# The first expert's extra rows ahead of its gate, and linear attention with unmasked keys: one layer of a hybrid diffusion block on one Trainium2 core

## The chip, the core and the metric

The kernel runs on one core of one Trainium2 chip. The metric is device time in microseconds, from launch to end, as the median of several runs. Of the kernel before there are three runs: 1279.64, 1281.47 and 1281.56 us, so the median is 1281.47 us. One execution was also taken with the hardware profiler; all views below come from that one.

## The reference, cut to what matters

256 tokens of width 1024 and 256 context tokens go through one layer, in float32. First a mixer: a combined input projection (`w_in`), then two branches, a bidirectional chunked gated linear attention (4 heads, keys of 64, values of 128, chunks of 64 tokens) and a latent attention, a merge with sigmoid gates, and an output projection. Then a mixture of 32 experts, of which each token takes its top 4.

```python
ds = jnp.einsum("bhncd,bhnce->bhnde", k_to_end, vc)      # state added by one chunk of 64 tokens
def step(s, inp):
    d, dsn = inp
    return d[..., None] * s + dsn, s
...
merged = jax.nn.sigmoid(f["zm_gla"]) * br_gla + jax.nn.sigmoid(f["zm_mla"]) * br_mla
...
mod_x = jnp.split((jax.nn.silu(c) @ w_mod[l] + b_mod[l])[:, None, :], 6, axis=-1)
...
for e in range(N_EXPERTS):
    gate = jnp.minimum(tok @ p["w_gate"][e] + p["b_gate"][e], SWIGLU_LIMIT)
    up = jnp.clip(tok @ p["w_up"][e] + p["b_up"][e], -SWIGLU_LIMIT, SWIGLU_LIMIT)
    act = (up + 1.0) * gate * jax.nn.sigmoid(SWIGLU_ALPHA * gate)
    out = out + combine[:, e:e + 1] * (act @ p["w_down"][e] + p["b_down"][e])
```

## The kernel before, in words

**Loads.** Nearly all weights come in pieces of 2 MB, issued by SyncE (SP) in its program order. In the mixer the class `Slots` (L90) holds three slots; `PLAN` (L27) says which piece goes into which slot and in which order, and `done(name)` frees a slot and issues what is next for it (L115). All four pieces `g0` to `g3` of the modulation weights use slot 2, one after the other. For the experts the class `Ring` (L48) has ten slots: each expert has two pieces of its gate, two of its up and two of its down projection, and `done(n)` frees the n oldest pieces and issues as many new ones (L75), each of which waits for TensorE's last read of its slot.

**Mixer.** `work()` (L604) yields the projection products piece by piece; each `Q(...)` (L864) in the linear attention flushes stored evacuations, runs one such product step (24 matmuls of 256 columns, high and low parts of the split weights), splits the next weights (`wsh` on ScalarE L365, `wsl` on VectorE L366), and may then take one half of a `g` piece: `mod_part` (L313) scales 2 times 128x1024 on ScalarE (L322) and adds them on GpSimd (L324). TensorE, VectorE, ScalarE, GpSimd and SP follow the written order there.

Linear attention: `decays(t)` (L911) makes the decay factors and the keys `kx`, one masked tile for each chunk with the other chunk's 64 rows at zero (L930 to L932); `states(i)` (L944) multiplies keys and values chunk by chunk and adds to the running state (L954); `queries`, `scores`, `inner`, `outer` follow. The order of the stretch is: decays(0), Q, decays(1), Q, states(0), queries(0), states(1), Q, states(2), then scores and inner products with Qs between them. Halves of `g1` are taken by the second and third Q, those of `g2` by two Qs after `queries(1)`. `on_pool` (L846) prepares the bias rows `RB` on GpSimd.

**Experts.** Tokens of an expert are gathered into 64 slots; an expert with more than 64 tokens has 32 extra rows, under `tc.If(rv > 0)`, where `rv` is loaded by every engine from the tile `trips` (L1573, L1589). `project` (L1437) multiplies gathered rows with the pieces, `gated` and `upped` evacuate, `turn` transposes, `down` multiplies with the down pieces, `scatter` adds to the output accumulators. Expert 0 is written out by hand (L1613 to L1645): main gate products with the extra rows' gather between them, `table()`, the slots' tokens, the gate, then the extra rows' gate products in two halves, each of which frees one piece; likewise up and down. Experts 1 to 31 (L1647 to L1656): gate, up, then under the `If` the extra rows' gather, gate and up, and only then `ring.done(4)`; after the down products `ring.done(2)`. After expert 20 a loop for crowded experts is skipped over (`crowded`, L1534).

Of the kernel before, what the change touches and what calls it, by code (L numbers as in the profile page):

```python
# [17 lines left out]
D = 1024  # L18
# [4 lines left out]
EB = 2  # L23
LIMIT = 7.0
# [103 lines left out]
def block_kernel(ctx: ExitStack, tc: tile.TileContext, a, out):  # L128
# [185 lines left out]
    def mod_part(name, jj, done=True):  # L314

        c, acc, first = int(name[1]), sums[name[0]], name[1] == "0" and jj == 0
        if jj == 0:
            sums[name] = ring.take(name)
        w = sums[name][:, jj]
        for n in range(2):  # L320
            v, to = w[:, ts(n, 1024)], acc[:, ts(n, 1024)]
            nc.scalar.activation(to if first else v, v, AF.Identity, scale=cz[:, 2 * c + jj, 0:1])  # L322
            if not first:
                nc.gpsimd.tensor_add(to, to, v)  # L324
        if jj == 1 and done:
            ring.done(name)
# [285 lines left out]
    def work():  # L612
# [22 lines left out]
        for n in range(6):  # L635
# [203 lines left out]
    kx = [[place(2, 1536 + 1024 * t + 512 * c, 512, 2) for c in range(2)] for t in range(2)]  # L839
# [3 lines left out]
    bias_dma = nc.sync.dma_start(bias[:96], a["b_gu"].rearrange("k p n -> p k n"))  # L843
    side = []

    def on_pool():  # L846

        nc.gpsimd.memset(RB, 0.0)
        yield
        for k in range(2):  # L850
            for h in range(2):
                v, part = bias[:, k, ts(h, 512)], RB[:, k, ts(h, 512)]
                mid, low = slice(32, 64), slice(64, 96)
# [36 lines left out]
    for t in range(2):  # L890
        for c in range(2):
            nc.gpsimd.memset(kx[t][c][64 * (1 - c):64 * (1 - c) + 64], 0.0)
# [20 lines left out]
    def decays(t):  # L913
# [16 lines left out]
        for c in range(2):  # L930
            r = slice(64 * c, 64 * c + 64)
            nc.vector.tensor_mul(kx[t][c][r], er[r], zk[r, t:t + 1].to_broadcast([64, 2, 256]))  # L932
# [3 lines left out]
    Q(1, "g1:0")  # L936
# [4 lines left out]
    Q(1, "g1:1")  # L941


    def states(i):  # L944
        ps_ = []
        for d in range(2):
            c = i if d == 0 else 3 - i
            p = bank(f"p_ds{d}{i}", (128, 2, 2, 128))
            ds_mm(p, kx[c // 2][c % 2], c // 2, d, None, None)
            ps_.append((p, c))  # L950
# [20 lines left out]
    last_e = nc.scalar.activation(sg, zg, AF.Sigmoid)  # L971
# [55 lines left out]
    Q(1)  # L1027
    inner(0, 0)
    scores(0, 1)
    Q(1)  # L1030
# [75 lines left out]
    for b, o, name in ((1, om, "w_br_mla"), (0, og, "w_br_gla")):  # L1106
        w = w_br.pop(name, None) or ring.take(name)
        for c in range(4):
# [8 lines left out]
            with tc.issue_after(last_e.ins):  # L1117
                nc.scalar.activation(v, v, AF.Sigmoid)
# [26 lines left out]
    comb3 = late.tile([128, 2, 96], F32, name="comb3")  # L1145
# [180 lines left out]
    def slot_ids(at, slots):  # L1326

        return iota[:, at:at + slots].unsqueeze(1).to_broadcast([128, 128 // slots, slots])

    def select(G, i, e):  # L1330

        for t in range(2):
            nc.vector.tensor_scalar(G[:, t, i], slot_ids(0, SLOTS), posm[:, t, e:e + 1], r2[t], op0=ALU.is_equal, op1=ALU.mult)

    def gather(X, G, g):

        p = bankb("p_xg", (128, 4, SLOTS * EB))
        for k in range(4):
            for t in range(2):
                mm(p[:, k], x1[:, t, ts(4 * g + k, 128)], G[:, t, :, 0], t == 0, t == 1)  # L1340
# [8 lines left out]
    def gather_one(X, G, i):  # L1349

        p = bankb("p_xg")
        for t in range(2):
            for q in range(2):
                mm(p[SLOTS * q:SLOTS * q + SLOTS], G[:, t, i, 0], x1[:, t, ts(q, 512)], t == 0, t == 1)
        yield
        xg = [mo.tile([128, 512], F32, tag=n, name="xg")[:, :256] for n in "su"]
# [20 lines left out]
    def table():  # L1377
# [5 lines left out]
        for t in range(2):  # L1383
            nc.tensor.transpose(p[:96, 2 + t], comb3[:, t], C("ident"))
        q = p.rearrange("p a b -> p (a b)")
        v, part = q[:, 256:], where[:, 256:]
        mid, low = slice(32, 64), slice(64, 96)
        nc.scalar.copy(where[:32, :256], q[:32, :256])
        nc.vector.tensor_copy(part[:96], v[:96])
        nc.vector.tensor_sub(part[mid], v[mid], part[mid])  # L1390
        nc.vector.tensor_sub(v[low], v[low], part[low])
        nc.vector.tensor_copy(part[low], v[low])
# [15 lines left out]
    def block_tiles():  # L1408
        return (mo.tile([128, 2, EB, 128 // SLOTS, SLOTS], F32, tag="G", name="G"),
                mo.tile([128, 8, EB * SLOTS], F32, tag="X", bufs=2, name="X"))  # L1410

    def more_gather(at, posm, tag="1"):

        rep = 128 // MORE
        G = mo.tile([128, 2, rep, MORE], F32, tag="G" + tag, name="G")
        for t in range(2):
            nc.vector.tensor_scalar(G[:, t], slot_ids(at, MORE), posm[:, t], r2[t], op0=ALU.is_equal, op1=ALU.mult)
        yield None
        p = bankb("p_xg", (128, D // rep))
        for t in range(2):  # L1420
            for q in range(rep):
                mm(p[MORE * q:MORE * q + MORE], G[:, t, 0], x1[:, t, ts(q, D // rep)], t == 0, t == 1)
        xg = mo.tile([128, 512], F32, tag="s", name="xg")[:, :D // rep]
# [35 lines left out]
    def more_bank(k):  # L1459
        return bankb(f"p_m{k}", (128, 256))  # L1460
# [11 lines left out]
    def more_in(of, X, W, w):  # L1472

        p = more_bank(0)
        project(0, p, of, X, 0, W, MORE)
        g = more_gated(p, w)
        p = more_bank(1)
        project(1, p, of, X, 0, W, MORE)
        return more_upped(p, g)
# [46 lines left out]
    def more_out(S, ps_, ns=range(2)):  # L1526

        ys = [halves(p, (("g", "s"), ("u", "y1"))[n]) for n, p in zip(ns, ps_)]
# [3 lines left out]
    def crowded():  # L1532

        with tc.If(worst > 1):  # L1534
            with tc.For_i(0, NE, 1) as ev:
# [8 lines left out]
                with tc.For_i(1, rv, 1):  # L1544
# [9 lines left out]
                    u2 = more_in(se, X2, lambda c, j: rows_from(("w_gate", "w_up")[c // 2], 4 * (c % 2) + j), w2)  # L1554
# [7 lines left out]
    select(G, 0, 0)  # L1562
    first = gather_one(X, G, 0)
    next(first)
# [9 lines left out]
    steps = [more_gather(SLOTS, posm[:, :, 0:1])]  # L1574
    next(steps[0])
    next(first)
    next(first)
    softmax(0, 1)
    softmax(1, 1)
    nc.vector.tensor_copy(comb3.rearrange("p t (c e) -> p t c e", c=3), comb.unsqueeze(2).to_broadcast([128, 2, 3, 32]))  # L1580
    select(G, 1, 1)
    chain.__exit__(None, None, None)
    ctx.enter_context(tc.manual_schedule(engines={E.PE}))
# [15 lines left out]
    for e in range(NE):  # L1599
# [12 lines left out]
        u = mo.tile([128, 512], F32, tag="u", name="u")  # L1612
        if e == 0:  # L1613

            project(0, p, of, X, 0, W, SLOTS, range(0, 4))
            steps.append(next(steps[0]))
            project(0, p, of, X, 0, W, SLOTS, range(4, 6))
            X1 = next(steps[0])
            table()
            project(0, p, of, X, 0, W, SLOTS, range(6, 8))  # L1620
            toks[0] = slot_tokens(of, first_sid)
            gated(p, g, toks[0][1])
            p1 = more_bank(0)
            for half in range(2):
                with tc.If(rv > 0):
                    if half == 0:
                        S1, w1 = slot_tokens(of, more_sid, "1")
                    project(0, p1, of, X1, 0, W, MORE, range(4 * half, 4 * half + 4))
                    if half:
                        g1 = more_gated(p1, w1)  # L1630
                ring.done(1)
                rv = blocks(e, ring.last.ins)
            p = bankb("p_up", tag="g")
            p1 = more_bank(1)
            for half in range(2):
# [8 lines left out]
                ring.done(1)  # L1644
                rv = blocks(e, ring.last.ins)  # L1645
        else:
            project(0, p, of, X, SLOTS * i, W, SLOTS)  # L1647
            gated(p, g, toks[e][1])
            p = bankb("p_up", tag="g")
            project(1, p, of, X, SLOTS * i, W, SLOTS)  # L1650
            upped(p, g, u)
            with tc.If(rv > 0):  # L1652
                X1 = list(more_gather(SLOTS, posm[:, :, e:e + 1]))[-1]
                S1, w1 = slot_tokens(of, more_sid, "1")
                u1 = more_in(of, X1, W, w1)
            ring.done(4)  # L1656
        following = list(range(e - i + EB, e - i + 2 * EB))
        if e and following[0] < NE:
# [5 lines left out]
            if i == 1:  # L1664
                gather(Xn, Gn, 1)
        aT = turn(u, SLOTS)
        if e:
            scatter(*todo)
        else:
            nxt = gather_one(X, G, 1)  # L1670
            for _ in range(3):
                next(nxt)
# [218 lines left out]
```

## Time and profile before

| | us |
|---|---|
| median of three runs | 1281.47 (1279.64 to 1281.56) |
| the profiled execution, device time | 1282.0 |
| its span, first to last instruction | 1280.1 |
| TensorE matmuls busy | 1153.5 (90% of the span) |
| VectorE, ScalarE, GpSimd busy | 420.8, 255.6, 133.5 |
| read from memory | 460.27 MB |

The span starts with the first instruction; 1.9 us of the execution lie around it. Times in the views are microseconds from the span's start. A busy TensorE is not TensorE at its peak; what counts in a stretch is which wait ends last there.

### The profile page before, as it was taken

The numbers are of one execution on the slowest core, as the hardware profiler recorded it, in microseconds if no ns is written. First come the engines' busy times: TensorE is split into PE (matmuls) and PEld (weight loads), VectorE is DVE, ScalarE is ACT, GpSimd is POOL, SyncE is SP. The second block draws the span as 40 slices with busy tenths as digits, with TensorE's granted clock in tenths as the row PEclk, the third lists the DMA queues.
The fourth block names the chain that finished last, engine by engine and source line by source line (L and its number), as shares of the span: only waits on it lengthen the run. The fifth ranks groups of instructions, "written<-read, shape, count | busy, mean of one in ns | idle before, by whom it ended". The sixth has DMA issues, their size and how long they took to land. (4 is left out here: it accounts for less than half of the span.)

```text
span 1280.1 us, 16131 instructions
## 1 busy us (share of the span) xinstructions
PE 1153.5 (90%) x6486; PEld 612.0 (48%) x6487; DVE 420.8 (33%) x784; ACT 255.6 (20%) x437; POOL 133.5 (10%) x93
## 2 busy tenths in 40 slices
PE   8999979999899999998988899998969889999984
PEld 5776768886344444443433343443524334444421
DVE  5667576685421222211111222221212111121212
ACT  4556534543111010110001010100101000110101
POOL 2346236540000000000000000000000000000000
PEclk9999989999999999999999999999989999999997
DMA  9843445896669999999999999999889999999993
GB/s 364 321 167 112 193 154 191 344 352 269 264 233 425 426 426 426 425 425 428 425 426 427 427 425 425 426 425 426 378 372 425 427 425 428 424 427 426 425 413 128
DMA packets 37988, 463.24 MB, mean 362 GB/s; under 512 B 4600, under 2 KB 4856, under 8 KB 10336
## 3 DMA queue, kind: packets, MB, share of 16 engines
q1 hardware_dynamic: 37424, 461.16, 86.6%
q8 instruction: 100, 1.64, 0.5%
q14 instruction: 32, 0.26, 0.1%
q10 hardware_dynamic: 432, 0.18, 0.1%
HBM read 460.27 MB, written 1.05 MB: 360 GB/s over the span
## 5 line engine op out<-in xcount | busy, mean ns | idle before, releaser
L203 PE MATMUL p_up<-w,X 128*64 128x512 f32 x1024 | 229.5, 594 | 15.8 <-DMA w<-in_w_up_dram 15.8
L203 PE MATMUL p_y<-w,aT 128*64 128x512 f32 (+1 forms) x1088 | 236.1, 599 | 1.0 <-ACT aT L1487 1.0
L203 PE MATMUL p_gate<-w,X 128*64 128x512 f32 x1024 | 230.1, 597 | 3.3 <-DMA w<-in_w_gate_dram 3.3
L203 PEld LDWEIGHTS p_up<-w,X 128*64 128x64 f32 x1024 | 88.5, 137 | 144.6 <-issue 111.6
L203 PEld LDWEIGHTS p_gate<-w,X 128*64 128x64 f32 x1024 | 95.7, 138 | 114.4 <-issue 108.1
L203 PEld LDWEIGHTS p_y<-w,aT 128*64 128x64 f32 (+1 forms) x1088 | 72.7, 136 | 144.0 <-issue 141.3
L213 POOL TENSOR_TENSOR rx<-rx,cst 128x1 f32<-128x1 f32 x2 | 1.5, 770 | 965.3 <-DVE rx L212 965.3
L1510 DVE TENSOR_TENSOR yl<-p_y,yh 128x512 fp32r<-128x512 f32 x33 | 22.8, 691 | 227.6 <-ACT yh L1509 227.6
L1451 DVE TENSOR_SCALAR g<-p_gate 128x512 f32<-128x512 f32 x32 | 22.1, 692 | 218.5 <-PE p_gate L203 218.5
L203 PE MATMUL p_xg<-G,x 128*128 128x128 f32 x480 | 64.8, 290 | 32.0 <-PEq L1652 20.4
L203 PEld LDWEIGHTS p_xg<-G,x 128*128 128x128 f32 x480 | 59.2, 200 | 56.9 <-issue 56.9
L1487 ACT COPY aT<-p_aT 128x512 f32<-128x512 f32 (+1 forms) x34 | 19.5, 575 | 322.7 <-PE p_aT L1485 322.7
L1456 DVE TENSOR_SCALAR u<-p_up 128x512 f32<-128x512 f32 x32 | 22.1, 692 | 171.6 <-PE p_up L203 171.6
L1452 ACT ACTIVATE s<-g 128x512 f32<-128x512 f32 (+1 forms) x34 | 21.0, 617 | 285.7 <-DVE g L1451 285.7
L1509 ACT CAST yh<-p_y 128x512 fp32r<-128x512 f32 x33 | 19.4, 587 | 212.9 <-PEq L1709 199.6
L203 PE MATMUL p_gate<-h0h,wsl 128*128 128x256 f32 x160 | 47.1, 294 | 4.5 <-DVE wsl L366 4.3
L203 PEld LDWEIGHTS <-selb 128*64 128x64 bf16 (+2 forms) x178 | 15.4, 104 | 72.9 <-issue 67.4
L203 PE MATMUL p_gate<-h0h,wsh 128*128 128x256 f32 x160 | 48.7, 304 | 0.0
L1346 DVE TENSOR_SCALAR X<-p_xg,mA_gpref,mB_gpref 128x128 f32<-128x128 f32 x60 | 24.6, 410 | 71.8 <-PE p_xg L203 53.7
L203 PE MATMUL p_gate<-h0l,wsh 128*128 128x256 f32 x160 | 46.8, 292 | 0.0
L324 POOL TENSOR_TENSOR sums<-sums,g 128x1024 f32<-128x1024 f32 x14 | 37.2, 2682 | 60.4 <-ACT g L322 60.4
L366 DVE TENSOR_TENSOR wsl<-p,wsh 128x1024 fp32r<-128x1024 f32 x27 | 39.4, 1462 | 9.8 <-ACT wsh L365 9.7
(437 smaller groups left out, 1480.0 us busy)
## 6 DMA issues: line engine op xcount, KB each, us to landing
w<-in_w_gate_dram SPq DMA_DIRECT2D x64, 2048.0 KB, 35.8
w<-in_w_up_dram SPq DMA_DIRECT2D x62, 2048.0 KB, 35.8
w<-in_w_down_dram SPq DMA_DIRECT2D x62, 2048.0 KB, 27.9
p<-in_w_in_dram SPq DMA_DIRECT2D x7, 2048.0 KB, 9.6
a<-in_w_mod_a_dram SPq DMA_DIRECT2D x8, 1024.0 KB, 9.6
f<-in_w_mod_f_dram SPq DMA_DIRECT2D x4, 2048.0 KB, 8.6
g<-in_w_mod_g_dram SPq DMA_DIRECT2D x4, 2048.0 KB, 7.9
wo<-in_w_out_dram SPq DMA_DIRECT2D x2, 2048.0 KB, 12.9
```

The source lines that it names most:

```text
L203: nc.tensor.matmul(o, l, r, start=start, stop=stop)
L213: nc.gpsimd.tensor_tensor(dst, dst, C("nhalf")[:, :dst.shape[1]], op=ALU.pow)
L324: nc.gpsimd.tensor_add(to, to, v)
L366: (eng or nc.vector).tensor_sub(lo, src, hi.bitcast(F32))
L1346: nc.vector.tensor_scalar(X[:, j], p[:, k], fA[:, 0, j:j + 1], fB[:, 0, j:j + 1], op0=ALU.mult, op1=ALU.add)
L1451: nc.vector.tensor_scalar(g, pg, LIMIT, None, op0=ALU.min)
L1452: nc.scalar.activation(s, g, AF.Sigmoid, scale=ALPHA)
L1456: nc.vector.tensor_scalar(u, pu, LIMIT, -LIMIT, op0=ALU.min, op1=ALU.max)
L1487: nc.scalar.copy(aT, p)
L1509: nc.scalar.copy(hi, p)
L1510: nc.vector.tensor_sub(lo, p, hi.bitcast(F32))
```

## The change

In the mixer: the sums of the `g` pieces go from ScalarE and GpSimd to VectorE, two instructions for each half; the halves of `g1` are taken later, after `scores(0, 0)` and `scores(0, 1)`; the keys `kx` are one unmasked tile for two chunks, and `states` multiplies 64 rows of it; the merge gates are evacuated by a sigmoid on ScalarE instead of a copy on VectorE and a later sigmoid; the bias rows use four groups of 32 partitions and share their steps between ScalarE and GpSimd. In the experts: expert 0 gathers its extra rows before its gate, and takes the extra gate products between the main ones; experts 1 to 9 (`EARLY`) take the extra rows' gate under an `If` between gate and up, and free two pieces after the gate and two after up.

```diff
+EARLY = 10
@@ mod_part
-            nc.scalar.activation(to if first else v, v, AF.Identity, scale=cz[:, 2 * c + jj, 0:1])
+            by = cz[:, 2 * c + jj, 0:1]
+            if name[0] == "g" and not first:
+                nc.vector.scalar_tensor_tensor(to, v, by, to, op0=ALU.mult, op1=ALU.add)
+                continue
+            nc.scalar.activation(to if first else v, v, AF.Identity, scale=by)
@@ work: gate
-                    nc.vector.tensor_copy(to, p)
+                    if n:
+                        nc.scalar.activation(to, p, AF.Sigmoid)
+                    else:
+                        nc.vector.tensor_copy(to, p)
@@ linear attention
-    kx = [[place(2, 1536 + 1024 * t + 512 * c, 512, 2) for c in range(2)] for t in range(2)]
+    kx = [place(2, 1536 + 1024 * t, 512, 2) for t in range(2)]
@@ on_pool
-        nc.gpsimd.memset(RB, 0.0)
...
-                nc.gpsimd.tensor_copy(part[:96], v[:96])
+                nc.scalar.copy(part, v)
                 yield
-                nc.gpsimd.tensor_sub(part[mid], v[mid], part[mid])
-                nc.gpsimd.tensor_sub(v[low], v[low], part[low])
+                nc.gpsimd.tensor_sub(v[rest], v[rest], part[rest])
                 yield
-                nc.gpsimd.tensor_copy(part[low], v[low])
+                nc.scalar.copy(part[rest], v[rest])
+                yield
                 nc.gpsimd.tensor_sub(part[low], v[low], part[low])
@@ decays
-        for c in range(2):
-            r = slice(64 * c, 64 * c + 64)
-            nc.vector.tensor_mul(kx[t][c][r], er[r], zk[r, t:t + 1].to_broadcast([64, 2, 256]))
+        nc.vector.tensor_mul(kx[t], er, zk[:, t:t + 1].to_broadcast([128, 2, 256]))
@@ order
     ee = [decays(0)]
-    Q(1, "g1:0")
+    Q(1)
     ee.append(decays(1))
...
-    Q(1, "g1:1")
+    Q(1)
@@ states
-            ds_mm(p, kx[c // 2][c % 2], c // 2, d, None, None)
+        for pr in range(2):
+            for d, (p, c) in enumerate(ps_):
+                r = slice(64 * (c % 2), 64 * (c % 2) + 64)
+                for h in range(2):
+                    hd = 2 * pr + h
+                    mm(p[64 * h:64 * h + 64, d, pr], kx[c // 2][r, d, 64 * hd:64 * hd + 64],
+                       gv[r, c // 2, ts(hd, 128)], True, True)
@@ order
     scores(0, 0)
-    Q(1)
+    Q(1, "g1:0")
     inner(0, 0)
     scores(0, 1)
-    Q(1)
+    Q(1, "g1:1")
     inner(0, 1)
     outer(0)
     queries(1)
     Q(1, "g2:0")
@@ merge
-                nc.scalar.activation(v, v, AF.Sigmoid)
@@ before the experts
     select(G, 0, 0)
+    more = more_gather(SLOTS, posm[:, :, 0:1])
+    next(more)
     first = gather_one(X, G, 0)
+    next(first)
+    next(more)
+    next(first)
+    next(more)
     next(first)
 ...
     nc.vector.tensor_copy(trips[:, :32], count)
@@ expert 0
             project(0, p, of, X, 0, W, SLOTS, range(0, 4))
+            X1 = list(more)[-1]
+            softmax(0, 1)
+            softmax(1, 1)
...
             project(0, p, of, X, 0, W, SLOTS, range(4, 6))
+            chain.__exit__(None, None, None)
+            p1 = more_bank(0, "g")
+            with tc.If(rv > 0):
+                project(0, p1, of, X1, 0, W, MORE, range(0, 4))
+            rv = freed(1)
+            project(0, p, of, X, 0, W, SLOTS, range(6, 8))
             table()
+            with tc.If(rv > 0):
+                project(0, p1, of, X1, 0, W, MORE, range(4, 8))
+                S1, w1 = slot_tokens(of, more_sid, "1")
+                g1 = more_gated(p1, w1)
+            rv = freed(1)
             toks[0] = slot_tokens(of, first_sid)
             gated(p, g, toks[0][1])
             p = bankb("p_up", tag="g")
+            p1 = more_bank(1, "g")
@@ experts 1 to 31
             project(0, p, of, X, SLOTS * i, W, SLOTS)
             gated(p, g, toks[e][1])
+            if early:
+                with tc.If(rv > 0):
+                    X1, S1, g1 = more_first()
+                rv = freed(2)
             p = bankb("p_up", tag="g")
             project(1, p, of, X, SLOTS * i, W, SLOTS)
             upped(p, g, u)
...
-            ring.done(4)
+            if early:
+                rv = freed(2)
+            else:
+                ring.done(4)
```

`freed(n)` is `ring.done(n)` and a new load of `rv` placed after the transfers on SP. In expert 0 the gather of expert 1's rows also starts before `turn` instead of after it.

## Rows read from the trace of the kernel before

**Rows 1.** Busy time by window: stretch, us; PE, PEld, DVE, ACT, POOL; clock; DMA share; GB/s

```profile
364.00:376.00 12.00, 11.69 (x60) 4.23 (x57) 2.53 (x4) 0.63 (x1) 0.00 (x0) 1.00 0.10 33
...
500.00:600.00 100.00, 91.63 (x470) 41.48 (x468) 22.36 (x47) 9.89 (x19) 0.00 (x0) 1.00 1.01 426
```

**Rows 2.** Waits of TensorE over the whole span: us in total, times, longest

```profile
PE p_xg L203 <- PEq L1652: 20.4, 23, 3.3
PE p_up L203 <- DMA w<-in_w_up_dram: 15.8, 16, 1.9
...
PE p_gate L203 <- PEq L1589: 8.3, 1, 8.3
PE p_ds L203 <- DVE place L932: 5.5, 1, 5.5
...
PE p_gate L203 <- DVE wsl L366: 4.3, 2, 2.8
...
PE pm_g L203 <- POOL sums L324: 1.7, 1, 1.7
...
PE p_st L203 <- ACT X L1369: 0.9, 1, 0.9
```

**Rows 3.** Timeline of SP: issues of the experts' pieces, 374 to 388 us

```profile
374.96 1.44 SPq L75 DMA_DIRECT2D w<-in_w_down_dram  x2
...
387.99 0.94 SPq L75 DMA_DIRECT2D w<-in_w_up_dram  x2
```

**Rows 4.** Timeline of TensorE: main products of expert 1, gate of expert 9

```profile
360.71 7.03 PE L203 MATMUL p_gate<-w,X 128*64 128x512 f32 x32
...
380.76 7.09 PE L203 MATMUL p_y<-w,aT 128*64 128x512 f32 x32
...
575.02 7.19 PE L203 MATMUL p_gate<-w,X 128*64 128x512 f32 x32
```

**Rows 5.** Timeline of all engines in the linear attention

```profile
157.28 1.38 DVE L932 TENSOR_TENSOR place<-er,place 64x512 f32<-64x512 f32 x2
...
165.42 6.03 DVE L932 TENSOR_TENSOR place<-er,place 64x512 f32<-64x512 f32 x2
165.50 0.66 PE L203 MATMUL p_ds<-place,place 128*64 128x128 f32 x8
166.28 4.63 POOL L324 TENSOR_TENSOR sums<-sums,g 128x1024 f32<-128x1024 f32 x2
```

**Rows 6.** Busy time by window, the tile p_gate alone, at both clocks

```profile
157.00:159.00 2.00, 2.00 (x19) 1.95 (x17) 0.00 (x0) 1.00 0.99 426
176.00:178.00 2.00, 2.00 (x11) 2.00 (x11) 0.00 (x0) 0.50 1.05 451
```

**Rows 7.** The pieces g: issue of g2 on SP, and issue to landing

```profile
170.93 0.35 SPq L115 DMA_DIRECT2D g<-in_w_mod_g_dram  x1
...
DMA to landing us min/median/max: 7.8/7.9/8.0
```

**Rows 8.** Timeline of VectorE: an instruction of the new kind, two of half the size

```profile
302.87 1.42 DVE L1206 SCALAR_TENSOR_TENSOR x<-v,rx,x 128x512 f32<-128x512 f32 x2
```

**Rows 9.** Timeline of VectorE, TensorE and ScalarE in expert 0

```profile
310.70 0.17 DVE L1570 CAST trips<-count 1x32 int32<-1x32 f32 x1
...
313.32 3.65 PE L203 MATMUL p_gate<-w,X 128*64 128x512 f32 x16
320.57 1.94 PE L203 MATMUL p_gate<-w,X 128*64 128x512 f32 x8
...
323.33 1.28 ACT L1452 ACT_TABLE_LOAD   x1 [2.23 <-DVE g L1451]
324.62 0.63 ACT L1452 ACTIVATE s<-g 128x512 f32<-128x512 f32 x1
324.69 0.60 PE L203 MATMUL p_st<-where,selb 128*128 128x512 bf16 x2 [2.18 <-DVE where L1393]
...
329.79 0.41 PE L203 MATMUL p_up<-RB,selb 128*64 128x512 bf16 x2
```

More of the change, by code (lines that the diff above doesn't have):

```diff
@@ L1612, in block_kernel, with freed @@
         u = mo.tile([128, 512], F32, tag="u", name="u")
+        def freed(n):
+            ring.done(n)
+            return blocks(e, ring.last.ins)
         if e == 0:
             project(0, p, of, X, 0, W, SLOTS, range(0, 4))
-            steps.append(next(steps[0]))
-            project(0, p, of, X, 0, W, SLOTS, range(4, 6))
-            X1 = next(steps[0])
-            table()
-            project(0, p, of, X, 0, W, SLOTS, range(6, 8))
+            X1 = list(more)[-1]
+            softmax(0, 1)
+            softmax(1, 1)
+            nc.vector.tensor_copy(comb4.rearrange("p t (c e) -> p t c e", c=4),
+                                  comb.unsqueeze(2).to_broadcast([128, 2, 4, 32]))
+            select(G, 1, 1)
+            project(0, p, of, X, 0, W, SLOTS, range(4, 6))
+            chain.__exit__(None, None, None)
+            ctx.enter_context(tc.manual_schedule(engines={E.PE}))
+            p1 = more_bank(0, "g")
[3 more added lines that the diff above has]
+            project(0, p, of, X, 0, W, SLOTS, range(6, 8))
+            table()
+            with tc.If(rv > 0):
[3 more added lines that the diff above has]
+            rv = freed(1)
             toks[0] = slot_tokens(of, first_sid)
             gated(p, g, toks[0][1])
[L1623 to L1632, printed above, removed]
             p = bankb("p_up", tag="g")
-            p1 = more_bank(1)
+            p1 = more_bank(1, "g")
             for half in range(2):
@@ L1643, in block_kernel, with more_first @@
                         u1 = more_upped(p1, g1)
-                ring.done(1)
-                rv = blocks(e, ring.last.ins)
+                rv = freed(1)
         else:
+            early = e < EARLY
             project(0, p, of, X, SLOTS * i, W, SLOTS)
             gated(p, g, toks[e][1])
+            def more_first():
+                X1 = list(more_gather(SLOTS, posm[:, :, e:e + 1]))[-1]
+                S1, w1 = slot_tokens(of, more_sid, "1")
+                return X1, S1, more_in(0, of, X1, W, w1)
+            if early:
+                with tc.If(rv > 0):
+                    X1, S1, g1 = more_first()
+                rv = freed(2)
             p = bankb("p_up", tag="g")
@@ L1669, in block_kernel @@
         else:
-            nxt = gather_one(X, G, 1)
-            for _ in range(3):
-                next(nxt)
+            next(nxt)
         if e + 1 < NE:
@@ L1703, in block_kernel @@
                         more_out(S1, ps_)
-                ring.done(1)
-                if half == 0:
-                    rv = blocks(e, ring.last.ins)
+                rv = freed(1)
         elif e < NE - 1:
@@ L1779, in _constants @@
     sel = np.zeros((n, 32))
-    for k in range(96):
-        sel[k, k % 32] = 1
+    for k in range(n):
+        sel[k, k % 32] = not 32 <= k < 64
     c["sel"] = sel
```

95 lines of the change are left out of this document (39 added, 56 removed).

## The prediction

> **What bounds the kernel now.** I read the windows first. From about 375 us to the end the transfers set the pace: in a plain stretch of the experts the DMA engines are busy throughout at 426 GB/s [rows 1], and TensorE, though 92% busy, waits for pieces of weights [rows 2]. A piece of 2 MB takes 2.097/0.426 = 4.92 us, an expert's six 29.5 us, while TensorE gets from expert 1 to expert 9 in (575.0 - 360.7)/8 = 26.8 us each [rows 4]. So the end comes when the stream of pieces ends, plus an unchanged tail; time is gained only by starting the unbroken stream earlier.
>
> What starts it? The ring's ten slots are full before expert 0 is done; then each transfer waits for TensorE. From 364 to 376 us the DMA engines idle (share 0.10) [rows 1]: expert 1's gate products end at 360.71 + 7.03 = 367.7 [rows 4], but their two slots are freed together with those of up, at 374.96 [rows 3]. From there the stream is unbroken. Ahead of it TensorE sets the pace, with its waits in the mixer. The longest is 5.5 us in the linear attention [rows 2]: two masked key products on VectorE, 0.69 us each undisturbed, take 6.03 us while two adds run on GpSimd [rows 5]. After that wait the granted clock stands at 0.50 (1.2 instead of 2.4 GHz), and TensorE passes 11 projection matmuls in 2 us instead of 19 [rows 6].
>
> **Part A: g1 leaves the decays.** Without GpSimd's adds the second key product is ready before TensorE wants it, so the wait of 5.5 us goes, and with it the 1.5 us for a split weight just before (4.3 us in two times, the longest 2.8) [rows 2]. With them goes the half clock: it covered one product step of 24 matmuls, 24 x (2/11 - 2/19) = 1.8 us, and some 3 us of state products at half pace, so 1.5 us. Part A takes away 5.5 + 1.5 + 1.8 + 1.5 = 10.3 us. The keys as one instruction save 0.7 us of VectorE, hidden behind TensorE: nothing. The merge gates' sigmoids read PSUM directly: ScalarE does as many, VectorE copies less, and both are hidden by the product steps; if the cover fails, an evacuation costs 0.6 us [rows 9]. The 64-row state products I cost as before, 8 in 0.66 us [rows 5]. The Trainium skill, "TensorEngine Tiling (Array Packing)", Theoretical Speedup, gives up to 2x where the contraction is at most 64; by it some 1.5 us more would go. No row of this trace has 64-row products interleaved like this.
>
> **Part B: where g1 and g2 land.** A half of g is now two VectorE instructions of 128x1024. The nearest row is 0.71 us for 128x512 [rows 8], so about 1.25 each, 2.5 a half, queued ahead of the scores' evacuations. Worse, g1 and g2 share a slot: g2 is issued when g1's last half is summed (170.93 before) and lands 7.9 us later [rows 7]. Before, four Qs lay between that sum and the first use of g2; now none does, only inner, outer and `queries(1)`. VectorE has some 3 us of its own after g1:1 and then waits about 5 us for the landing; the evacuation of scores(1, 0) is queued behind. TensorE meanwhile has the rest of one product step (2 us), the scores (1) and another step (24 x 2/19 = 2.5, nearer 3 with its start), about 6. The evacuation is there 7.9 + 2.5 + 0.6 = 11 us after g1:1, so TensorE stands at inner(1, 0) for 5.0 us. A like wait cost a half clock of 3.3 us in Part A, and I take it again. What goes there is the 2.8 us wait for a split weight [rows 2] and its own short spell at half clock, which I put at 1.8. Net loss 5.0 + 3.3 - 2.8 - 1.8 = 3.7 us. Bounds: a gain of 4.6 us where the landing is covered; a loss of 12 us where most of VectorE's seven halves (17.5 us) ends on TensorE's path. I take 3.7, from the landing's own row.
>
> **Part C: the end of the mixer.** TensorE's wait of 1.7 us for GpSimd's last sum [rows 2] goes. The bias rows' copies on ScalarE now wait for GpSimd in between and stand ahead of a weight split; that may cost 0 to 2 us, and I take 0, as TensorE has a product step and the sums' products to cover it. The mixer in all: 10.3 - 3.7 + 1.7 = 8.3 us, and all up to expert 1 moves with it.
>
> **Part D: expert 0.** The extra rows' gather now stands ahead of `trips` on VectorE, and TensorE's load of `rv` keeps its written place before the gate. I put `trips` some 4.8 us later than 310.70, behind one selection and six evacuations, and so the first gate products at 316.1 instead of 313.32 [rows 9], 2.8 us late. By the end of the extra gate products this is made good, as the wait of 2.18 us for the table and a shorter one behind it [rows 9] are filled with products. Then a new wait: up takes the PSUM buffer of the main gate, whose evacuation now stands behind the extra rows' gate. From the table's transposes at about 327.6: table 2.3 (an estimate: from 320.57 to 324.69 it took 4.1 with the main gate's minimum in it [rows 9]), minimum 0.4, activation table 1.28, sigmoid 0.4, product 0.5, branch and load 0.5, minimum 0.7: 6.1 us, the small ones estimated from the 0.63 of a full sigmoid [rows 9]. So up starts at 333.7 instead of 329.79 [rows 9], 3.9 us late. Expert 1's rows gathered ahead of `turn` give back 0.9 [rows 2]; crossing the new `If` in expert 1 costs 20.4/23 = 0.9 [rows 2]. TensorE is 3.0 us late at expert 1's gate and 3.9 at its down; bounds 0 and 7, with the waits for `trips` and for the buffer not there or both in full. The activation table load takes 1.28 us and the sigmoid starts right behind it [rows 9]. The Trainium skill, "ScalarE: Activation LUTs", What ACT_TABLE_LOAD costs, adds a drain of 1.38 us to each switch; by it up would start 1.4 us later still. The row decides.
>
> **Part E: early frees.** Expert 1's gate slots are freed at 367.7 + 3.0 = 370.7, its up slots before they are due, and four pieces end at 370.7 + 19.7 = 390.4. The down slots are freed at 388.0 + 3.9 = 391.9 [rows 3], and two pieces end at 401.7. Before, six pieces from 374.96 ended at 404.5. So the stream is 2.8 us ahead, and expert 2's early frees (at about 399.6) come before it runs dry. Expert 0's first piece is freed earlier too, but the stream stands idle again before 370, so that is worth nothing. The nine new crossings are hidden while an expert's 26.8 us stays under 29.5.
>
> **Sum.** 8.3 + 2.8 = 11.1 us, from the profiled execution's 1282.0 to 1270.9; the median stands 0.5 lower, so **1270.4 us**. About 0.2% (2.6 us) is what a measurement of this kernel can tell from no change.
>
> **Rivals.** (1) *The landing is covered.* If TensorE has more to do before inner(1, 0), or g1:1 ends earlier, 5.0 + 3.3 us of Part B go: 1262.1. For: the DMA engines have little to do there. Against: every piece g took 7.8 to 8.0 us [rows 7]. Chance 0.2. (2) *Half of it is lost.* VectorE bounds the scores (Part B at 8 us) and expert 0 is at its late bound (Part E near 0): 1270.4 + 4.3 + 2.8 = 1277.5. For: VectorE's queue is long there; against: TensorE has a product step in each Q. Chance 0.16. (3) *Slower: the new crossings.* TensorE waits at the end of an `If` up to 3.3 us, 0.9 on average, and 8.3 us once, behind the crowded loop [rows 2]. Nine more stand between gate and up of experts 1 to 9. With c each, an expert takes 26.8 + c, and above 29.5 the stream runs dry: the loss is 8 x (c - 2.7) less 2.1 us of slack, which eats the gain from c = 4.4 on; at 5.5 the time is 1270.4 + 20.3 = 1290.7, at 8.3 it is 1313. For: that one crossing of 8.3. Against: the other 23. Chance 0.08. (4) *It does not do what it says:* front and mixer give back what they gain, with Part B at its bound of 12 us and Part E at 0: 1270.4 + 8.3 + 2.8 = 1281.5. Chance 0.06.
>
> **How the numbers follow.** The forecast has 0.5, with 1265 to 1275 around it. Rival 1 reaches down to 1260.5, rival 2 up to 1277.5; they make the range, and rivals 3 and 4 are left out. Faster by over 0.2%: 0.5 + 0.2 + 0.16 = 0.86; within 0.2%: 0.06; slower: 0.08.
>
> **What would show it.** Right: no wait of 5 us at the state products, clock 1.00 there; VectorE waiting for g2 with TensorE idle at inner(1, 0); the first gate products behind a late `trips`; up waiting for a PSUM buffer; the stream unbroken from about 362 (370.7 less 8.3), at the same 426 GB/s. Wrong: DMA gaps inside experts 2 to 9, which would mean that the crossings bound; or an end that stays although the stream starts earlier.

## The result, and the profile after

The changed kernel takes **1266.41 us** (median of four runs, 1265.23 to 1267.63) against 1280.57 us for the kernel before (1279.64 to 1281.56, four runs): a ratio of 0.989, with an interval of 0.9876 to 0.9904, or 14.2 us less. The forecast was 1270.4 us, with 1260.5 to 1277.5 around it. The profiled execution took 1266.84 us with a span of 1265.1 us, 15.0 us under the span before.

Where the time went is best read by setting the same TensorE instruction of both traces side by side. Each row is the start of one instruction (the seventh row an issue of SP) in us; "lead" is how much earlier it comes in the changed kernel.

| place | before | after | lead | forecast lead |
|---|---|---|---|---|
| decay sums ahead of the linear attention (`p_rc`) | 146.79 | 144.59 | 2.2 | 0 |
| first product of the Q behind `scores(0, 0)` (Part A) | 182.32 | 168.40 | 13.9 | 10.3 |
| first product behind the half clock of Part B (`p_og`) | 209.15 | 200.46 | 8.7 | 6.6 |
| a product of the merge (`p_br<-ogh,wsl`; Part C) | 269.55 | 259.35 | 10.2 | 8.3 |
| expert 0's first up product (`p_up`) | 329.79 | 320.76 | 9.0 | 4.4 |
| expert 1's gate products | 360.71 | 351.04 | 9.7 | 5.3 |
| expert 1's down slots freed | 387.99 | 379.46 | 8.5 | 4.4 |
| end of the span | 1280.1 | 1265.1 | 15.0 | 11.1 |

The waits of TensorE over the whole span, in us in total, times and longest, stand against [rows 2]:

```profile
PE p_aT L1480 <- PEq L1666: 5.3, 1, 5.3
PE p_up L204 <- PEq L1660: 4.7, 9, 0.5
PE po L204 <- DVE at L988: 4.6, 2, 4.4
...
PE p_gate L204 <- DVE trips L1576: 2.0, 1, 2.0
...
PE p_at L204 <- DVE on L1016: 1.6, 1, 1.6
...
PE p_gate L204 <- DVE wsl L371: 0.9, 2, 0.4
```

The wait of 5.5 us at the state products is gone, and so are the wait for GpSimd's last sum and most of that for split weights. Three are new: 4.4 us at the inner products (`po`), 1.6 us at the scores (`p_at`), 2.0 us for `trips`. The nine new crossings (L1660) cost 0.5 us each.

Parts A and B, in the timelines of VectorE and TensorE, beside [rows 5]:

```profile
155.12 0.69 DVE L933 TENSOR_TENSOR place<-er,place 128x512 f32<-128x512 f32 x1
...
159.72 0.69 DVE L933 TENSOR_TENSOR place<-er,place 128x512 f32<-128x512 f32 x1
...
187.66 2.48 DVE L325 SCALAR_TENSOR_TENSOR sums<-g,cz,sums 128x1024 f32<-128x1024 f32 x2 [4.93 <-DMA g<-in_w_mod_g_dram]
...
190.12 0.75 DVE L988 SCALAR_TENSOR_TENSOR at<-p_at,place 128x256 f32<-128x256 f32 x2
...
191.92 2.48 DVE L325 SCALAR_TENSOR_TENSOR sums<-g,cz,sums 128x1024 f32<-128x1024 f32 x2
194.31 0.69 DVE L1016 TENSOR_TENSOR on<-po,ro 128x512 f32<-128x512 f32 x1
```

```profile
161.53 0.89 PE L204 MATMUL p_ds<-place,place 64*64 64x128 f32 x20
162.99 0.65 PE L204 MATMUL p_ds<-place,place 64*64 64x128 f32 x12 [0.57 <-DVE st L958]
166.63 0.67 PE L204 MATMUL p_ds<-place,place 64*64 64x128 f32 x16
...
190.60 2.08 PE L204 MATMUL po<-place,at 128*128 128x128 f32 x8 [4.41 <-DVE at L988]
...
195.15 1.19 PE L204 MATMUL p_at<-qx,e 128*128 128x256 f32 x2 [1.62 <-DVE on L1016]
```

Each key product takes 0.69 us, long before the state products at 161.53. Part B follows: VectorE stands 4.93 us for the landing of g2, the evacuation of `scores(1, 0)` (L988) is queued behind the two sums, and TensorE waits 4.41 us for it. The second half of g2 then holds up `on` (L1016), which the forecast had not priced. SP's timeline gives the cause, and the early frees to set against [rows 3] and the 170.93 of [rows 7]:

```profile
179.81 0.33 SPq L116 DMA_DIRECT2D g<-in_w_mod_g_dram  x1
...
358.21 0.80 SPq L76 DMA_DIRECT2D w<-in_w_down_dram  x2
...
379.46 0.87 SPq L76 DMA_DIRECT2D w<-in_w_up_dram  x2
```

The piece g2 is issued at 179.81 and used at 187.66, 7.85 us later. The clock behind the wait, by windows with the tile `p_gate` alone (columns as in [rows 6]), and the experts by windows as in [rows 1]:

```profile
196.00:198.00 2.00, 2.00 (x9) 1.91 (x10) 0.00 (x0) 0.00 (x0) 0.50 0.00 0
```

```profile
361.00:376.00 15.00, 14.29 (x87) 8.09 (x85) 4.83 (x13) 2.32 (x5) 0.00 (x0) 1.00 1.01 428
500.00:600.00 100.00, 93.49 (x478) 42.72 (x476) 21.34 (x46) 9.86 (x19) 0.00 (x0) 1.00 1.01 426
```

The granted clock is 0.50 (1.2 GHz) behind the wait. The DMA engines, idle from 364 to 376 us before, are busy there, and in the plain stretch they move the same 426 GB/s. TensorE's timeline gives the experts' pace, beside [rows 4]: (571.22 - 351.04)/8 = 27.5 us for an expert, where it was 26.8, still under the 29.5 us of six pieces.

```profile
351.04 7.03 PE L204 MATMUL p_gate<-w,X 128*64 128x512 f32 x32
...
571.22 7.09 PE L204 MATMUL p_gate<-w,X 128*64 128x512 f32 x32
```

Expert 0, beside [rows 9], by the timelines of VectorE and then of TensorE:

```profile
304.74 0.14 DVE L1576 CAST trips<-most 1x1 int32<-1x1 f32 x1
...
316.83 0.69 DVE L1449 TENSOR_SCALAR g<-p_gate 128x512 f32<-128x512 f32 x1 [2.07 <-PE p_gate L204]
```

```profile
305.17 0.66 PE L204 MATMUL p_gate<-RB,selb 128*64 128x512 bf16 x2 [2.02 <-DVE trips L1576]
305.51 5.22 PE L204 MATMUL p_gate<-w,X 128*64 128x512 f32 x16
...
320.76 0.41 PE L204 MATMUL p_up<-RB,selb 128*64 128x512 bf16 x2
```

By windows, all instructions (PE, PEld, DVE, ACT, POOL; clock; DMA share; GB/s):

```profile
306.00:308.00 2.00, 2.00 (x6) 0.68 (x4) 0.00 (x0) 0.00 (x0) 0.00 (x0) 0.50 0.00 0
```

`trips` is late, as forecast, and behind that wait of 2.02 us the granted clock stands at 0.50 once more: the first 16 gate products take 5.22 us, where they took 3.65 before [rows 9]. That is 1.6 us which the forecast had not priced. It does not always come: in a second profile of the same kernel (`after_again`, below) the wait is 2.02 us too, the clock stays at 1.00 and the 16 products take 3.65 us. The main gate's minimum (`g<-p_gate`), against the forecast, runs right behind the last gate product, ahead of the table, and up waits for no buffer.

### The profile page after: what moved, and what is told of

It is laid out like the page before. It is cut to its first block, busy times and chain, and to the rows that moved or that the text cites. A ratio compares the mean times of both kernels' runs of the same rounds, so it can differ in the third digit from the quotient of the medians.

```text
span 1265.1 us, 16274 instructions
## 1 busy us (share of the span) xinstructions
PE 1148.6 (91%) x6484; PEld 603.1 (48%) x6487; DVE 405.5 (32%) x787; ACT 246.6 (19%) x432; POOL 79.6 (6%) x62
## 5 line engine op out<-in xcount | busy, mean ns | idle before, releaser
L371 DVE TENSOR_TENSOR wsl<-p,wsh 128x1024 fp32r<-128x1024 f32 x27 | 36.1, 1335 | 13.1 <-ACT wsh L370 13.0
L204 PE MATMUL p_gate<-RB,selb 128*64 128x512 bf16 x64 | 14.3, 403 | 26.3 <-PEq L1726 15.6
```

The lines of the kernel that those rows point to most:

```text
L204: nc.tensor.matmul(o, l, r, start=start, stop=stop)
L371: (eng or nc.vector).tensor_sub(lo, src, hi.bitcast(F32))
```

## The experiments

All times are medians. The kernels were measured in three groups, each beside runs of the kernel before (medians 1280.29, 1283.28 and 1281.85 us), so kernels of different groups are compared by their ratios to it. Diffs are against the changed kernel, whose own ratio was 0.989 first and 0.9884 (0.9864 to 0.9903) when it was run again beside the last three. Ahead of the linear attention the start times scatter by some 3 us in profiles of the same code, so for the edits in the linear attention one stretch is given as well, from the start of the decay sums (`p_rc`) to that of `p_og`: 62.4 us before, 55.9 and 55.4 in the two profiles of the changed kernel.

**The two parts by themselves.** `mixer_alone` takes all the edits up to the end of the mixer (with the bias table of four groups) and leaves the experts as before; `experts_alone` is the reverse.

```diff
-EARLY = 10
...
-    more = more_gather(SLOTS, posm[:, :, 0:1])
-    next(more)
     first = gather_one(X, G, 0)
...
+            ring.done(4)
```

> The mixer's part of the change alone; the experts as before. Theory: TensorE reaches expert 0 some 10 us earlier, as in the changed kernel's trace, and since nothing in the experts is different the whole stream of pieces moves by as much, so 1270 to 1272 us. Rival: the mixer's gain is taken back in waits for pieces of weights ahead of expert 1, and most of the 14 us comes from the early frees: 1276 us or more.

Measured: 1274.00 us, ratio 0.9948 (0.9931 to 0.9966), 6.3 us less, between the theory and the rival. In the profiled execution, the fastest of the six at 1272.61 us, the first pieces are issued at 365.40 instead of 374.96, and the span is 9.3 us shorter than that of before; the others took up to 3 us more, so the size is less sure than the expectation had it.

```diff
-            if name[0] == "g" and not first:
-                nc.vector.scalar_tensor_tensor(to, v, by, to, op0=ALU.mult, op1=ALU.add)
-                continue
...
+        for c in range(2):
+            r = slice(64 * c, 64 * c + 64)
+            nc.vector.tensor_mul(kx[t][c][r], er[r], zk[r, t:t + 1].to_broadcast([64, 2, 256]))
```

> The experts' part of the change alone; the mixer as before. Theory: expert 1's gate slots are freed some 7 us before its up slots, its first products start 0.5 us later, and the stream gets 4 to 5 us ahead: 1275 to 1277 us, so that the two parts add up to the 14 us of both. Rival: the crossings and the late loop counts cost as much as the early frees give, 1280 us; or the front is worth little without the mixer's time, and the parts do not add up.

Measured: 1275.02 us, ratio 0.9955 (0.9938 to 0.9972), 5.3 us less. Neither part needs the other: together the medians give 11.6 us of the 14.2, and 0.9948 x 0.9955 = 0.990 lies within the interval of the whole change. In its trace TensorE is no earlier at expert 1's up than before (367.83 for 367.58), and yet the stream is, as SP's timeline shows: the first two pieces are issued at 367.34 instead of 374.96 [rows 3].

```profile
367.34 0.80 SPq L76 DMA_DIRECT2D w<-in_w_down_dram  x2
```

**The wait for g2.** Its halves are moved one product step, then two.

```diff
     queries(1)
-    Q(1, "g2:0")
+    Q(1)
     norm(0)
     scores(1, 0)
-    Q(1, "g2:1")
+    Q(1, "g2:0")
     normed_o(0)
     inner(1, 0)
     scores(1, 1)
-    Q(1)
+    Q(1, "g2:1")
     outputs(0)
```

> The changed kernel, but with each half of g2 taken one product step later, so that the wait for its landing is no longer ahead of the evacuation of scores(1, 0). Theory: the two waits of TensorE in front of the second tile's inner and score products (4.4 and 1.6 us) go, and with them the half clock behind them (some 3 us): 1257 to 1259 us. Rival: VectorE's queue is what bounds there, the two sums of 2.6 us show up as waits at the next inner products, and the time is 1263 us or more.

Measured: 1261.15 us, ratio 0.9841 (0.9814 to 0.9868). By the ratios a gain of 5 to 6 us, between the two theories; the stretch up to `p_og` takes 51.9 us, 3.5 to 3.9 less (the profiled execution was the slowest of the four, 1264.95 us). The wait has moved: `inner(1, 0)` goes through, but the sums still stand until the landing, now ahead of `on` (L1016), and the next scores wait for that. VectorE and then TensorE:

```profile
190.34 2.48 DVE L325 SCALAR_TENSOR_TENSOR sums<-g,cz,sums 128x1024 f32<-128x1024 f32 x2 [3.65 <-DMA g<-in_w_mod_g_dram]
```

```profile
193.56 0.67 PE L204 MATMUL p_at<-qx,e 128*128 128x256 f32 x2 [4.30 <-DVE on L1016]
```

```diff
     scores(1, 1)
-    Q(1)
+    Q(1, "g2:0")
     outputs(0)
     inner(1, 1)
     outer(1)
-    Q(1)
+    Q(1, "g2:1")
     norm(1)
```

> The changed kernel, but with the halves of g2 taken two product steps later (with one step the first half still waited for its landing, and the wait of 4.3 us stood at the next score products). Theory: g2 lands some 8.7 us after the last half of g1, and from there on nothing that TensorE needs is queued behind it on VectorE; the waits of 4.4 and 1.6 us and the half clock behind them go, 7 to 9 us: 1257 to 1260 us. Rival: VectorE's queue bounds there whatever the order, a wait of over 2 us stays, and the time is 1262 us or more.

(The first two Qs of the diff above stand without g2 here.) Measured: 1258.35 us, ratio 0.9804 (0.9785 to 0.9823), by the ratios some 10 us under the changed kernel. No wait of TensorE over 0.6 us is left between 140 and 240 us; the stretch up to `p_og` takes 45.9 us, 9.5 to 9.9 less. VectorE had room for the sums all along: what Part B lost was the landing of g2 and the half clock behind it.

**Why g1's place mattered.** `g1_in_decays` puts g1 back behind the decays, still on VectorE; `g1_decays_pool` also gives the sums back to ScalarE and GpSimd.

```diff
     ee = [decays(0)]
-    Q(1)
+    Q(1, "g1:0")
     ee.append(decays(1))
...
-    Q(1)
+    Q(1, "g1:1")
...
     scores(0, 0)
-    Q(1, "g1:0")
+    Q(1)
     inner(0, 0)
     scores(0, 1)
-    Q(1, "g1:1")
+    Q(1)
```

> The changed kernel with the halves of g1 back at their old places, behind the two decays, but still summed on VectorE. Theory (GpSimd's adds beside the key product made the wait of 5.5 us, and the landing of g2 makes the new one): no wait of 5 us at the state products, VectorE's four sums of 1.3 us cost TensorE 0 to 4 us there, g2 lands before it is wanted, and 4 to 9 us are gained: 1257 to 1262 us. Rival (the place was the reason, VectorE has no room there): a wait of 5 us and a half clock at the state products as before, 1266 us or more.

Measured: 1264.90 us, ratio 0.9855 (0.9834 to 0.9875), between the theory and the rival. By the ratios that is some 4 us under the changed kernel, but its interval overlaps that of 0.9884, and the medians are only 1.3 us apart (1266.22). The stretch up to `p_og` is clearer: 52.1 us, 3.3 to 3.8 less. The sums do cost TensorE time there (3.6 us, with a half clock behind them), since the state update (L958) is queued behind them, but less, by that stretch, than the landing of g2 costs in the changed kernel:

```profile
PE p_ds L204 <- DVE st L958: 3.6, 1, 3.6
PE p_at L204 <- DVE on L1016: 1.3, 1, 1.3
```

```diff
-            if name[0] == "g" and not first:
-                nc.vector.scalar_tensor_tensor(to, v, by, to, op0=ALU.mult, op1=ALU.add)
-                continue
...
-    Q(1)
+    Q(1, "g1:0")
...
```

> The changed kernel with g summed on ScalarE and GpSimd again and g1 at its old places, so that of the mixer's part the unmasked keys, the sigmoids and the bias rows are left. Theory: the key product, one instruction instead of two, still runs beside GpSimd's adds and takes 2 to 3 us instead of 0.7, so TensorE waits 2 to 4 us at the state products, and the waits for a split weight and for the last sum come back: 1270 to 1276 us. Rival: one key product instead of two is enough to take the wait of 5.5 us away, and as g2 lands early the time is below the changed kernel's, 1260 to 1264 us.

Measured: 1274.51 us, ratio 0.9929 (0.9912 to 0.9945), 5 to 6 us above the changed kernel by the ratios, as the theory had it, but not by its mechanism. The key product (L930) takes 0.68 us; the instructions that suffer stand on either side of it: the decay product ahead (L929; the same two take 0.76 us in the changed kernel), which makes the key product late, and the split of a weight behind (L368), 1.22 us by itself. VectorE, GpSimd and TensorE:

```profile
161.12 3.64 DVE L929 TENSOR_TENSOR e<-e,place 128x256 f32<-128x256 f32 x2 [1.42 <-ACT e L922]
164.68 0.68 DVE L930 TENSOR_TENSOR place<-er,place 128x512 f32<-128x512 f32 x1
...
165.88 5.70 DVE L368 TENSOR_TENSOR wsl<-p,wsh 128x1024 fp32r<-128x1024 f32 x1
```

```profile
159.06 5.41 POOL L326 TENSOR_TENSOR sums<-sums,g 128x1024 f32<-128x1024 f32 x2 [11.01 <-ACT g L324]
...
165.88 4.62 POOL L326 TENSOR_TENSOR sums<-sums,g 128x1024 f32<-128x1024 f32 x2
```

```profile
165.50 0.87 PE L204 MATMUL p_ds<-place,place 64*64 64x128 f32 x16 [1.50 <-DVE place L930]
172.25 1.12 PE L204 MATMUL p_ds<-place,place 64*64 64x128 f32 x12 [5.87 <-DVE st L955]
```

The split starts with GpSimd's adds at 165.88 and ends at 171.58, 1.08 us after they end at 170.50: that fits an instruction that does its work when they are through, and not one that runs beside them at a lower pace. TensorE waits 1.50 + 5.87 = 7.4 us at the state products, so the unmasked keys alone take no wait away. With the sums on VectorE at the same place 3.6 us of it are left (`g1_in_decays`), and moving g1 takes those. `experts_alone` (0.9955) differs from this kernel by the keys, the sigmoids and the bias rows; the two intervals overlap, so what these three are worth by themselves is not shown.

**The buffer that up should have waited for.** VectorE is held to the written order from the table to the main gate, so that the main gate's minimum stands behind the extra rows' gate.

```diff
+            written = tc.manual_schedule(engines={E.PE, E.DVE})
+            written.__enter__()
             table()
...
             gated(p, g, toks[0][1])
+            written.__exit__(None, None, None)
```

> The changed kernel with VectorE held to the written order from the table to the main gate of expert 0, so that the main gate's minimum stands behind the extra rows' gate. Theory: the up products then wait for the main gate's PSUM buffer, some 4 to 5 us, as the prediction had it, and the stream starts by as much later: 1269 to 1272 us. Rival: up waits, but the time is made good before the down slots are freed, 1266 to 1267 us.

Measured: 1269.29 us, ratio 0.9884 (0.9868 to 0.9901), no different from the changed kernel. The median lies in the theory's range, but the kernel before took 1283.28 us in this group, and from the first gate products to expert 1's first freed pieces this trace takes 53.7 us, and the changed kernel's 53.0. Both theories are wrong: up hardly waits. VectorE and TensorE:

```profile
323.11 0.42 DVE L1449 TENSOR_SCALAR g<-p_m 128x256 f32<-128x256 f32 x1
...
326.83 0.69 DVE L1449 TENSOR_SCALAR g<-p_gate 128x512 f32<-128x512 f32 x1
```

```profile
323.59 0.41 PE L204 MATMUL p_up<-RB,selb 128*64 128x512 bf16 x2 [0.67 <-DVE g L1449]
...
327.57 0.29 PE L204 MATMUL p_m<-RB,selb 128*32 128x256 bf16 x4
```

Up starts at 323.59, 3.2 us ahead of the main gate's minimum: it takes the buffer that the extra rows' gate has just left. The main gate's goes to the extra rows' up, which wants it only at 327.57.

**The early frees and their crossings.** `EARLY` is 1, 3 and 31 instead of 10, so that no expert behind expert 0, experts 1 and 2, or experts 1 to 30 free early.

```diff
-EARLY = 10
+EARLY = 1
```

> The changed kernel with no early frees in experts 1 to 9 (four pieces freed together after up, no new If between gate and up); expert 0 as changed. Theory: the unbroken stream then starts where the four pieces are freed, at about 365 us, and six pieces end some 9.7 us earlier than in the kernel before instead of 15.2, so 1271 to 1273 us. Rival: expert 0's earlier frees carry the gain, and the early frees of the others do nothing or cost their crossings: 1265 to 1267 us.

Measured: 1273.37 us, ratio 0.9934 (0.9913 to 0.9955), by the ratios 0.9934 - 0.989 = 0.0044, or 5.6 us of 1281, above the changed kernel. SP's timeline has the first pieces at 366.12, where the changed kernel issues two at 358.21. The six pieces so end at 366.12 + 29.5 = 395.6 instead of 389.3, 6.3 us later; that its last two are freed at 379.15, as early as in the changed kernel (379.46), hardly matters.

```profile
366.12 1.42 SPq L76 DMA_DIRECT2D w<-in_w_down_dram  x2
...
379.15 1.15 SPq L76 DMA_DIRECT2D w<-in_w_up_dram  x2
```

```diff
-EARLY = 10
+EARLY = 3
```

> The changed kernel with early frees in experts 1 and 2 only. Theory: in expert 3 four pieces are freed together when the stream has run dry for some 3.4 us (freed at about 422 us, while the pieces on their way end at about 419.7), and never again after that: 3 to 4 us above the changed kernel. Rival: only expert 1's frees matter, the same time as the changed kernel; or the stream falls behind in every expert from 3 to 9, over 5 us above.

Measured: 1270.23 us, ratio 0.991 (0.989 to 0.9931), 4.0 us above the changed kernel in the same group (1266.22). The stream runs dry once, where it was expected, as the window from 421 to 425 us shows (DMA share 0.48; it is 1.01 in the windows on either side):

```profile
421.00:425.00 4.00, 3.70 (x27) 2.51 (x24) 1.41 (x3) 0.00 (x0) 0.00 (x0) 1.00 0.48 135
```

The dry spell is worth 4 x 0.53/1.01 = 2.1 us. The rest is not the stream's: in this trace its first pieces are issued at 359.23, in the changed kernel's of this group at 356.55, behind the same code.

```diff
-EARLY = 10
+EARLY = 31
```

> The changed kernel with early frees and the second If in all experts from 1 to 30 instead of 1 to 9. Theory: each crossing costs TensorE 0.5 to 0.9 us, and as TensorE waits for pieces there, nothing comes of it: within 1.5 us of the changed kernel, with the waits for pieces shorter by as much as the crossings take. Rival: crossings add up where TensorE has no slack (the expert with extra rows, the last one), 3 us or more above it.

Measured: 1261.09 us, ratio 0.9835 (0.981 to 0.9859): 5.1 us below the changed kernel in the same group, where both theories had nothing or a loss. The stream ends no earlier: SP issues the last pieces at 1223.66, and at 1223.74 in the changed kernel. The gain is behind the stream, in the last expert, which the edit does not touch. TensorE's timeline of the changed kernel in this group, and then of this one:

```profile
1225.91 0.39 PE L204 MATMUL p_up<-RB,selb 128*64 128x512 bf16 x2
...
1239.05 1.08 PE L1480 MATMUL p_aT<-cst,u 128*128 128x128 f32 x4 [5.33 <-PEq L1666]
```

```profile
1225.86 0.39 PE L204 MATMUL p_up<-RB,selb 128*64 128x512 bf16 x2
...
1235.28 0.63 PE L1480 MATMUL p_aT<-cst,u 128*128 128x128 f32 x4 [1.61 <-DVEq L1733]
```

The last expert's up starts at the same time in both; past its `If` one waits 5.33 us and the other 1.61, and behind it the granted clock is 0.50 (from 1239 to 1243) in the one and 1.00 (from 1233 to 1240) in the other. The profile of the kernel before and all the others of this study have this wait, with 5.2 to 5.4 us.

**A better version.** The changed kernel as it is, and `both`: g2 two product steps later, and the loop counts ahead of the gather.

> The changed kernel unchanged, on the chip of the next three, as their base: 14 us below the kernel before.

Measured: 1266.22 us, ratio 0.9884 (0.9864 to 0.9903), 15.6 us less.

```diff
     select(G, 0, 0)
+    tf = late.tile([1, 32, 6], F32, name="tf")
...
+    nc.vector.tensor_copy(trips[:, 32:33], most)
     more = more_gather(SLOTS, posm[:, :, 0:1])
...
-    tf = late.tile([1, 32, 6], F32, name="tf")
...
```

> The changed kernel with the halves of g2 two product steps later, and with the loop counts (trips) worked out ahead of the gather of expert 0's rows instead of behind it. Theory: the wait of 2.0 us ahead of the first gate products goes as well as the waits for g2, and the stream starts some 10 us earlier than in the changed kernel: 9 to 11 us below it on this chip. Rival: the first gate products then wait for the gather's evacuations instead, or the time is lost again ahead of expert 1: 7 to 9 us below, as with g2 alone.

Measured: **1254.40 us**, ratio 0.9782 (0.9764 to 0.9799), 11.8 us below the changed kernel, a little more than the theory's 9 to 11. The wait for `trips` is gone too, and nothing takes its place, as TensorE's timeline shows (no idle time ahead of the first gate product, and 3.65 us for the 16 products behind it):

```profile
295.19 0.43 PE L204 MATMUL p_gate<-RB,selb 128*64 128x512 bf16 x2
295.40 3.65 PE L204 MATMUL p_gate<-w,X 128*64 128x512 f32 x16
```

TensorE starts expert 0 10.0 us earlier than in the changed kernel, and the span is 10.4 us shorter (1253.4 for 1263.8): in this kernel a us saved ahead of the stream is a us saved at the end. `both` together with `EARLY = 31` was not tried.

## Why the prediction was right, and where its sum was off

**What bounds.** Right. The stream is unbroken from about 360 us but for some 1 us at 380, up to the crowded loop, whose gap is as before, and every lead gained ahead of it arrives at the end: by the forecast's own formula the six pieces end at 379.46 + 9.84 = 389.3 instead of 404.5, 15.2 us ahead, and the span is 15.0 us shorter. `mixer_alone`, `early_1`, `early_3` and `both` all follow it.

**Ahead of the change.** TensorE is 2.2 us ahead before the linear attention begins, which no part of the sum had. It can be scatter: ten profiles with the same code up to there begin the decay sums between 144.59 and 147.75 us. 1.6 us of it comes at about 74 us, with a wait of 1.37 us for a split weight, which stands in the profile of before and in three others of the fourteen, with the mixer as before and as changed, and not in the rest. Some 0.4 us comes between 142 us and the decay sums, behind the place where g0's sums have left GpSimd, and `mixer_alone` gains it on `experts_alone` as well; whether that is the reason is not shown.

**Part A.** 11.7 us instead of 10.3. The wait, its half clock and the split weight went as forecast. The half clock was worth 0.5 us more than the prediction's count of products in windows gave: its product step took 5.36 us before (175.15 to 180.51) and takes 3.06 now (163.57 to 166.63), so 2.3 instead of 1.8. The other part is the 64-row products, costed as before: the 48 of them take 0.89 + 0.65 + 0.67 = 2.2 us, where 16 took 1.09 at full clock before, so 3.3 for 48. The Trainium skill, "TensorEngine Tiling (Array Packing)", Theoretical Speedup, has up to 2x for them; this trace agrees, with 1.5x, and the prediction's choice against it cost 1.1 us.

**Part B.** Right in mechanism: VectorE waits 4.93 us for g2, TensorE 4.41 (forecast 5.0), and the half clock follows. Mis-sized by 1.5 us: the lead falls by 5.2 us instead of 3.7, as the second half of g2 makes another wait of 1.62 us. `g2_two_later` shows that rival 1's 8 us were there to be had; in the change as it stands the landing isn't covered.

**Part C.** 1.5 us instead of 1.7 (the lead goes from 8.7 to 10.2 at the merge): the wait for the last sum is gone, and two waits of 0.4 us for split weights stand there now.

**Part D.** This is the step that failed: "up takes the PSUM buffer of the main gate, whose evacuation now stands behind the extra rows' gate". Neither half holds. From the end of the chain only TensorE keeps the written order, and the minimum ran first; and where VectorE is held to the written order (`written_order`), up takes the other buffer and waits 0.67 us. So up came 1.2 us late against the mixer's lead of 10.2 instead of 3.9, and expert 1's down 1.7 instead of 3.9. The wait for `trips` was 2.02 us (forecast 2.8), and the half clock behind it cost the 1.6 us that the forecast put at nothing.

**Part E.** Right: expert 1's frees give the gain (`early_1` loses 5.6 us without them), and those of experts 3 to 9 are needed as long as the stream has no slack (`early_3` loses 4.0, some 2 of it in the stream).

**The sum.** Ahead of the linear attention 2.2 us and Part A 1.4 more than forecast, Parts B and C 1.7 less, Part D 2.2 better: 4.1 us, from the forecast 11.1 to the 15.2 of the stream. The medians, which do not hang on one execution's scatter, put the whole at 14.2. That the forecast is no further off is in part luck: Part B lost more than forecast, and the error of Part D, which was one of mechanism, and that of Part A went the other way.

**The rivals.** 3 falls: a crossing between gate and up costs 0.5 us, far from the 4.4 from which it would have decided, and with thirty of them (`early_31`) the last pieces are issued at the same time. 2 and 4 fall with the leads in the table.

## What to carry to other kernels

Find the transfer stream that sets the end, and price a change by how much earlier that stream starts; a us gained ahead of it is a us at the end, and work behind it counts only in the tail. When a sum or a copy is moved past the point that frees a buffer, count the steps to the next use of that buffer: here two product steps were worth some 10 us. Before pricing a wait on a buffer, look up which engines are really held to the written order, and which of the buffers comes free first.

## What the runs showed of the hardware that was not expected

**VectorE and GpSimd take turns.** The prediction read the slow key products as running beside GpSimd's adds. In `g1_decays_pool` a split of 1.22 us takes 5.70 us and ends 1.08 us after the adds. The Trainium skill, "Trainium Architecture — The Big Picture", What this means for kernel authors, calls the port that the two share an exclusive lock and not a split of bandwidth; this trace agrees. Not every VectorE instruction is held: in the changed kernel one that reads PSUM runs 0.75 us from 70.92, while GpSimd adds, by the timelines of VectorE and GpSimd:

```profile
70.92 0.75 DVE L572 TENSOR_SCALAR place<-p_mv,rd 128x512 f32<-128x512 f32 x1 [1.20 <-PE p_mv L204]
```

```profile
66.94 8.34 POOL L329 TENSOR_TENSOR sums<-sums,f 128x1024 f32<-128x1024 f32 x3 [11.29 <-issue]
```

**A wait of 5.3 us past the last expert's `If`.** It stands on the tail in every profile but that of `early_31`. In the changed kernel it lasts from 1235.45 to 1240.72, and the trace has one packet of 16384 bytes on the instruction queue that starts inside it, at 1237.90. In all thirteen profiles with the wait such a packet starts 2.4 to 2.6 us into it. The Trainium skill, "Runtime: NRT & Kernel Launch", Instruction fetch mechanics, says that a taken branch whose target isn't loaded yet waits for its block of instructions; that would fit, and the place where the code of the last expert falls would then decide. In `early_31` such a packet starts at 1236.23, when TensorE is already past the place (its products there start at 1235.28). No run here moved that code by itself, so the cause stays open, and the 5.1 us of `early_31` may not survive another edit.
